# A streaming encoder layer: the first stage rebuilt, with shifts and scales by quarters and the index keys made in it

## Chip, cores and metric

One core of a Trainium2 chip runs the whole program. The metric is the device time of one execution in microseconds (us). Before the change it is 1277.1 us, the median of 3 runs (1276.33 to 1277.18).

## What is computed

One encoder layer over 1024 prompt tokens and 32 sample tokens (together T = 1056), D_MODEL = 1024, all in float32:

```python
mod = silu(c) @ w_ada + b_ada                    # per stream: c_prompt or c_sample
shift, scale, gate = split(mod, 3)
h = rms_norm(x, g_norm) * (1 + scale) + shift
z = h @ w_in                                     # q k v gate_a iq iw ik glu gate_b merge
score = sum_heads(w * relu(iq . ik))             # indexer; top-k keys per query
y_a = (attention over the selected keys * silu(gate_a)) @ w_a
y_b = (silu(layer_norm(depthwise_conv(ga * sigmoid(gb)))) * silu(gate_b)) @ w_b
x = x + gate * ((sigmoid(m_a) * y_a + sigmoid(m_b) * y_b) @ w_out)
```

followed by a last RMSNorm; k, v, ik and the conv state are outputs too. The indexer has 8 heads of 64 (iq, 512 columns of `w_in`), 64 columns of keys (ik) and 8 of weights (iw).

## The kernel before

All matrix products of the layer itself are made from pairs of rounded float32 numbers: an operand is split into a high part (`hh`, `wh`) and the rest (`hl`, `wl`), and three matmuls, hh.wh, hl.wh and hh.wl, replace one (`mm3`, L129 to L132). Everything of `z` is laid out with features on partitions and the 1056 tokens on columns.

**First stage** (L218 to L438). It makes hh and hl, 8 blocks j of 128 features by 1056 tokens, and the indexer's queries. x comes as 9 token tiles (`load_x`, L240). A tile is squared and summed (ACT, `sq_x`), its root and reciprocal are made (`scale_x`, L295: up to three tiles share the small steps), it is scaled in place (L313 on ACT, L315 on DVE or POOL), transposed in eight 128x128 pieces (`trans_x`, L320, into two PSUM banks `tx`) and copied to `xT` (L333).

Shift and scale are products of a vector with `w_ada`. `mod` (L345) goes by halves q of 512 features, by i (shift or scale) and by k (8 blocks of the contraction): 32 pieces, each with a stationary of 4 columns (`scf`) and 512 moving columns. 20 of them are float32 matmuls (L355); 12 are first split by `mod_pre` (L341, L342) and run as two rounded matmuls (L352, L353). `mod_out` (L361) turns the rows by transposes (L365) and leaves shift and scale per feature in `AB`.

```python
        nc.gpsimd.tensor_scalar(h, x, AB[:, j, 2:3], AB[:, j, 0:1], op0=OP.mult, op1=OP.add)
        nc.scalar.activation(hi, x, AF.Identity, bias=AB[:, j, 0:1], scale=AB[:, j, 2:3])
        nc.vector.tensor_sub(lo, h, f32(hi))
```

This is `h_of` (L374 to L379): for each block j and each of three parts of the tokens (f: 0 to 255, i: 256 to 767, t: 768 to 1023) h is made on POOL (L377), its rounded value on ACT (L378) and the rest on DVE (L379): 24 calls. `iq_mm` (L391) makes the queries of the first two of four 128-column blocks of iq, each in columns 256 to 767 (512 wide) and 768 to 1055 (288 wide).

The order of all this is written out by hand in two strings of steps: `LOADS` (L76) is the order in which SP issues the transfers, `ORDER` (L80) the order of the compute steps. PE, DVE and ACT run their instructions exactly in the order of the program; POOL's and SP's instructions are put in order by a scheduler. `LOADS` takes w_ada in pieces of 128 or 256 rows by 512 columns; 4 buffers hold x tiles, 4 hold blocks of w_ada.

**After the first stage** `iq_out` (L509) empties the queries from PSUM, `first_w` (L528) splits the weights of the index keys, and `Jobs` (L551) runs a list of products (L1363) one behind the other: the keys and iw (72 columns, `idx_done`), iq blocks 2 and 3, then K, V and all the other columns of `w_in`, most through `proj` (L538, matmuls L545). Between the k blocks of a job, `step` (L487) pops one small piece of other work: transposes, score products (`dots`), the convolution, the top-k search.

Of the kernel before, what the change touches and what calls it, by code (L numbers as in the profile page):

```python
# [107 lines left out]
def _build(tc, nc, a, o, top):  # L108
# [141 lines left out]
    iqraw = None  # L250
    for op, *i in LOADS:
        if op == "x":
            load_x(*i)
        elif op == "a":
            load_ada(*i)
        elif op == "q":
            iqraw = load_w([(w_in, C_IQ, 256)])
        else:
            ikraw = load_w([(w_in, C_IK, 64), (w_in, C_IW, 8)])

    rest = tl(stp, [128, 512], BF, "junk")
    nc.vector.memset(rest, 0.0)
    psS, psS_st = pool("psS", space=PSUM)
    p = tl(psS, [128, 512], F, "iq00")
    for i in range(WARM):
        nc.tensor.matmul(p, rest[:, 0:128], rest, start=True, stop=True)
    nc.vector.memset(scf, 0.0)
# [4 lines left out]
    nc.scalar.activation(sc, p.rearrange("p (s k) -> p k s", s=2), AF.Silu)  # L272
    bg_ = tl(stp, [128, 24], F, "bg_")

    def bias():
        p = misc([128, 24])
        nc.tensor.transpose(p, brow, ident[:24, :24])
        nc.vector.tensor_copy(bg_, p)
        nc.vector.tensor_scalar(bg_[:, 8:16], bg_[:, 8:16], 1.0, None, op0=OP.add)

    nc.gpsimd.memset(f32(scz), 0.0)

    IQC = ((0, 512), (512, NIQ - 512))
    iqps = {0: {}, 1: {}}
    xT = tl(stp, [128, KD, T], F, "xT")

    sums = {}
# [7 lines left out]
    def scale_x(tiles):  # L295

        w = len(tiles)
        v, sq, r, t = [tl(stp, [128, 3], F, n, 2) for n in ("vv", "rs_s", "rs_r", "rs_t")]
        v, sq, r, t = v[:, :w], sq[:, :w], r[:, :w], t[:, :w]
        if 8 in tiles:  # L300
            yield lambda: nc.vector.memset(v, 1.0)
        for c, i in enumerate(tiles):
            yield lambda c=c, i=i, n=tok(i): nc.vector.tensor_scalar(v[:n, c:c + 1], sums[i][:n], 1.0 / D, EPS,
                                                                     op0=OP.mult, op1=OP.add)
        yield lambda: nc.scalar.activation(sq, v, AF.Sqrt)
        yield lambda: nc.vector.reciprocal(r, sq)
        yield lambda: nc.vector.tensor_mul(t, r, r)
        yield lambda: nc.vector.tensor_mul(t, t, v)
        yield lambda: nc.vector.tensor_scalar(t, t, -0.5, 1.5, op0=OP.mult, op1=OP.add)
        yield lambda: nc.vector.tensor_mul(r, r, t)  # L310
        for c, i in enumerate(tiles):
            if XENG[i] == 2:
                yield lambda c=c, i=i, n=tok(i): nc.scalar.mul(xn[i][:n], xn[i][:n], r[:n, c:c + 1])  # L313
                continue
            yield lambda c=c, i=i, n=tok(i), e=(nc.vector, nc.gpsimd)[XENG[i]]: e.tensor_scalar(  # L315
                xn[i][:n], xn[i][:n], r[:n, c:c + 1], 1.0, op0=OP.mult, op1=OP.mult)
# [1415 lines left out]
```

## Time and profile before

| | |
|---|---|
| median of 3 runs | 1277.1 us |
| the profiled execution | 1275.99 us |
| its span, first to last instruction | 1274.2 us |
| PE busy | 1250.3 us (98%) |
| PEld (weight loads) | 1176.6 us (92%) |
| DVE busy | 900.2 us (71%) |
| ACT busy | 617.6 us (48%) |
| POOL busy | 196.0 us (15%) |
| granted TensorE clock, mean | 0.997 of full |

PE is the matrix engine, PEld its weight loads, DVE the vector engine, ACT the scalar engine, POOL GpSimd, SP the engine that issues most DMAs. "Busy" counts an engine from an instruction's start to its end; a matmul's end is modelled, and two that follow one another overlap, so the distance from one start to the next is what a matmul costs. A shape such as `128*72 128x352` is a stationary of 128 rows by 72 columns and an output of 128 partitions by 352 columns as the profile prints it.

### The profile page before, as it was taken

The numbers are of one execution on the slowest core, as the hardware profiler recorded it, in microseconds if no ns is written. First come the engines' busy times: TensorE is split into PE (matmuls) and PEld (weight loads), VectorE is DVE, ScalarE is ACT, GpSimd is POOL, SyncE is SP. The second block draws the span as 40 slices with busy tenths as digits, with TensorE's granted clock in tenths as the row PEclk, the third lists the DMA queues.
The fourth block names the chain that finished last, engine by engine and source line by source line (L and its number), as shares of the span: only waits on it lengthen the run. The fifth ranks groups of instructions, "written<-read, shape, count | busy, mean of one in ns | idle before, by whom it ended". The sixth has DMA issues, their size and how long they took to land.

```text
span 1274.2 us, 19148 instructions
## 1 busy us (share of the span) xinstructions
PE 1250.3 (98%) x7434; PEld 1176.6 (92%) x7434; DVE 900.2 (71%) x1435; ACT 617.6 (48%) x1142; POOL 196.0 (15%) x289
## 2 busy tenths in 40 slices
PE   7999999999999999999999999999999999999997
PEld 2589999999999999999999999999998889998785
DVE  4855547878898898879885558853258888775554
ACT  5645444566766666677213343341236776123322
POOL 3740111000000000100000000000023353311222
PEclk9999999999999999999999999999999999999998
DMA  9431222121222122221322421257123335645131
GB/s 339 138 102 50 85 68 85 51 102 52 72 80 68 69 68 85 75 78 52 117 103 102 164 107 41 79 174 267 56 75 88 96 108 193 204 150 176 65 133 67
DMA packets 110395, 136.38 MB, mean 107 GB/s; under 512 B 10667, under 2 KB 87715, under 8 KB 110176
## 3 DMA queue, kind: packets, MB, share of 16 engines
q1 hardware_dynamic: 99232, 100.62, 24.9%
q10 hardware_dynamic: 5872, 19.48, 3.8%
q0 software_dynamic: 5200, 15.05, 3.6%
q8 instruction: 58, 0.95, 0.3%
q14 instruction: 33, 0.27, 0.1%
HBM read 98.60 MB, written 36.54 MB: 106 GB/s over the span
## 4 chain that ended last, share of the span: by engine, by line
PE 94%; DMA 2%; POOL 1%; DVE 1%; ACT 1%; issue 0%; SPq 0%; ACTq 0%; DVEq 0%
PE proj L545 70%; PE PT L1284 2%; PE y L132 2%; PE y L130 2%; PE y L131 2%; PE O L130 1%; PE O L132 1%; PE O L131 1%; PE misc L743 1%; PE misc L744 1%; POOL h L377 1%; DMA ada<-in_w_ada_dram 1%; PE misc L132 1%; PE misc L131 1%; DMA xt<-in_x_prompt_dram 1%; PE misc L130 1%
## 5 line engine op out<-in xcount | busy, mean ns | idle before, releaser
L967 DVE SCALAR_TENSOR_TENSOR s<-u,vec,s 128x1086 f32<-128x1086 f32 x240 | 314.5, 1347 | 2.6
L545 PE MATMUL proj<-hh,wh 128*128 128x352 f32 x1440 | 312.8, 325 | 0.0
L545 PE MATMUL proj<-hh,wl 128*128 128x352 f32 x1440 | 310.3, 323 | 0.0
L545 PE MATMUL proj<-hl,wh 128*128 128x352 f32 x1440 | 309.8, 323 | 0.0
L545 PEld LDWEIGHTS proj<-hh,wh 128*128 128x128 f32 x1440 | 245.1, 189 | 1.9
L545 PEld LDWEIGHTS proj<-hh,wl 128*128 128x128 f32 x1440 | 246.8, 188 | 0.0
L545 PEld LDWEIGHTS proj<-hl,wh 128*128 128x128 f32 x1440 | 244.6, 188 | 0.0
L813 ACT ACTIVATE relu<-scores,cand 128x384 bf16<-128x384 f32 (+6 forms) x224 | 183.8, 823 | 72.2 <-DVE cand L828 69.5
L127 DVE TENSOR_TENSOR wl<-raw,wh 128x1024 fp32r<-128x1024 f32 (+1 forms) x84 | 100.7, 1202 | 79.8 <-ACT wh L126 78.6
L126 ACT CAST wh<-raw 128x1024 fp32r<-128x1024 f32 (+1 forms) x84 | 86.0, 1027 | 55.5 <-PE proj L545 43.8
L746 ACT ACTIVATE relu<-misc 128x384 f32<-128x384 f32 (+3 forms) x80 | 40.0, 524 | 63.4 <-PE misc L744 62.1
L757 DVE SCALAR_TENSOR_TENSOR scores<-relu,iws,scores 128x384 f32<-128x384 f32 (+3 forms) x70 | 43.7, 655 | 34.4 <-ACT relu L746 34.4
L126 ACT CAST u<-PT 128x512 fp32r<-128x512 f32 (+2 forms) x76 | 43.2, 572 | 45.0 <-PE PT L1284 42.6
L127 DVE TENSOR_TENSOR u<-PT,u 128x512 fp32r<-128x512 f32 (+2 forms) x76 | 50.6, 671 | 14.7 <-ACT u L126 14.3
L906 ACT ACTIVATE s<-proj 128x1056 f32<-128x1056 f32 x24 | 25.3, 1053 | 67.9 <-PE proj L545 67.9
L813 ACT ACTIVATION_READ_ACCUMULATOR relu<-scores,cand 128x1 f32 x224 | 42.4, 189 | 0.0
L545 PE MATMUL proj<-oa,wh 128*128 128x352 f32 x192 | 41.2, 323 | 0.0
L1264 POOL TENSOR_SCALAR E<-E,st 128x1024 f32<-128x1024 f32 (+4 forms) x36 | 33.7, 935 | 41.9 <-DVE st L1263 21.0
L545 PE MATMUL proj<-u,wh 128*128 128x352 f32 x192 | 38.6, 322 | 0.0
L1259 ACT ACTIVATE E<-E,st 128x1024 f32<-128x1024 f32 (+4 forms) x36 | 34.7, 964 | 7.9 <-DVE st L1252 7.8
L938 POOL DMA_DIRECT2D out_dram<-cvo x8 | 4.1, 517 | 216.5 <-ACT cvo L937 216.5
L888 POOL DMA_DIRECT2D mask_d<-relu x7 | 3.8, 549 | 209.2 <-ACT relu L887 209.2
(447 smaller groups left out, 2120.7 us busy)
## 6 DMA issues: line engine op xcount, KB each, us to landing
raw<-in_w_in_dram SPq DMA_DIRECT2D x24, 1024.0 KB, 5.3
raw<-in_w_in_dram SPq DMA_DIRECT2D x16, 512.0 KB, 5.1
ada<-in_w_ada_dram SPq DMA_DIRECT2D x24, 256.0 KB, 5.8
sma_d<-s ACTq DMA_DIRECT2D x8, 528.0 KB, 2.7
smb_d<-s ACTq DMA_DIRECT2D x8, 528.0 KB, 2.7
ga_d<-s ACTq DMA_DIRECT2D x8, 528.0 KB, 2.7
qh_d<-s ACTq DMA_DIRECT2D x8, 528.0 KB, 2.7
ql_d<-s SPq DMA_DIRECT2D x8, 528.0 KB, 2.8
```

What stands on the lines that cost most here:

```text
L126: nc.scalar.copy(hi, src)
L127: nc.vector.tensor_sub(lo, src, f32(hi))
L130: nc.tensor.matmul(out, ah, bh, start=first, stop=False)
L131: nc.tensor.matmul(out, ah, bl, start=False, stop=False)
L132: nc.tensor.matmul(out, al, bh, start=False, stop=last)
L545: nc.tensor.matmul(p[:n, c, :CH], a_[:, k, :n], b_(k, c), start=first, stop=last)
L746: nc.scalar.activation(r[:, :n], p[:, :n], AF.Relu, scale=0.125)
L757: nc.vector.scalar_tensor_tensor(acc, r[:, :n], w, acc, op0=OP.mult, op1=OP.add)
L813: nc.scalar.activation(scr[:, :s.shape[1]], s, AF.Sign, bias=f32(hold["cand"])[:, i:i + 1], accum_out=cnt[:, i:i + 1])
L967: nc.vector.scalar_tensor_tensor(d[:, :DW], u[:, k:k + DW], wj[:, k:k + 1], d[:, :DW], op0=OP.mult, op1=OP.add)
L1259: nc.scalar.activation(e, e, AF.Exp, bias=mn, scale=-1.0, accum_out=st[:, 1:2])
L1264: nc.gpsimd.tensor_scalar(e, e, st[:, 2:3], 1.0, op0=OP.mult, op1=OP.mult)
```

## The change

The first stage is written anew; what comes after it is the same but for the first jobs.

- Shift and scale go by quarters q of 256 features. One moving row holds 256 shift and 256 scale columns, and `w_ada` comes in eight blocks of 1 MB (q, g), each by two DMAs with rows of 1 KB. `mod` runs 8 groups of four float32 matmuls. Each of the four has a stationary of 32 columns (2 in use, the others zero) and writes another 32 partitions of one PSUM bank, with another k block. `mod_row` copies the bank, `mod_cols` sums the four parts and turns the rows by four matmuls with the 0/1 matrix `sel`. `mod_pre` and its splits are gone.
- h of the outer tokens (t and f) is made in one call for blocks 2 to 7 (part `tf`), so there are 18 parts instead of 24, and h may be made on DVE ("D") or POOL ("P").
- The index keys are made in the first stage (`k_mm`), in three parts of 352 columns, from weights that are loaded and split there. The second block of the queries (iq 1) leaves the stage and becomes the first job.
- Every instruction group is a step of `ORDER`. New steps `z:n` run n matmuls of zeros (`idle`); 21 in all.
- The root, the reciprocal and the scaling are done tile by tile.

```diff
-    def load_ada(q, i, k0, n=4):
+    def load_ada(q, g):
+        t = ada[q, g] = tl(stp, [128, 4, 2, 256], F, "ada", 4)
+        for i in range(2):
+            c = D * i + 256 * q
+            nc.sync.dma_start(t[:, :, i], w_ada[512 * g:512 * g + 512, c:c + 256].rearrange("(k p) c -> p k c", p=128))
-            nc.tensor.matmul(out, sch[:, k, :], h, start=k == 0, stop=False)
-            nc.tensor.matmul(out, scz[:, k, :], l, start=False, stop=k == KD - 1)
-        else:
-            nc.tensor.matmul(out, scf[:, k, :], ada[q, i, k], start=k == 0, stop=k == KD - 1)
+    def mod(q, g):
+        if g == 0:
+            pm[q] = tl(psS, [128, 512], F, "acc")
+        for j in range(4):
+            nc.tensor.matmul(pm[q][32 * j:32 * j + 32], scp[:, 4 * g + j, :], ada[q, g][:, j].rearrange("p i c -> p (i c)"),
+                             start=g == 0, stop=g == 1)
+    def mod_cols(q):
+        p = pm[q] = misc([128, 2, 2, 2])
+        for i in range(2):
+            for c in range(2):
+                nc.tensor.matmul(p[:, i, c, :], mrow[q][:, 256 * i + 128 * c:256 * i + 128 * c + 128], sel[:, 0, 0:2],
+                                 start=True, stop=True)
+    def h_of(p, j, e):
...
+        ENG[e].tensor_scalar(h, x, AB[:, j, 2:3], AB[:, j, 0:1], op0=OP.mult, op1=OP.add)
+    def k_mm(k, c):
+        wh, wl, _ = iqw["k"]
+        out, z = ikp[:72, c, :CH], slice(CH * c, CH * c + CH)
+        mm3(out, wh[:, k, :], wl[:, k, :], hh[:, k, z], hl[:, k, z], *turn_of("k", c))
+    def idle(n):
+        for i in range(n):
+            nc.tensor.matmul(ikp[:, 0, :], rest[:, 0:128], rest, start=True, stop=True)
...
-    iq_out(0, (0,))
-    first = first_w()
-    iq_out(0, (1,))
-    iq_out(1)
+    iq_out(0)
...
-    jobs = [("w", [(w_in, C_IK, 64), (w_in, C_IW, 8)], [(0, 72, idx_done)], 1, hrows),
+    jobs = [("w", None, [(0, 128, 1)], 1, hrows),
...
-    cache_ik()
-    side.append(cache_kT)
-    Jobs(jobs, first).run()
+    jobs = Jobs(jobs, iqw[1])
+    jobs.load(1)
+    load_caches()
+    idx_done(ikp)
+    side.extend([cache_ik, cache_kT])
```

Of the two strings one line each (`x:8` loads tile 8, `a:0,1` the block q=0, g=1 of w_ada; `m` is `mod`, `t` and `c` a transposed half tile and its copy, `h`, `i`, `l` the three operations of h, `q` and `k` queries and keys by block and part):

```diff
-x:2 a:0,0,0,1 x:3 a:0,1,0,1 a:0,0,4,1 a:0,1,4,2 x:4 x:8 x:5 a:1,0,0,1 x:7 a:1,1,0,2 x:6 a:1,0,4,1 q a:1,1,4,1 x:0
+x:8 x:2 x:3 x:4 a:0,0 x:5 a:0,1 x:6 k x:7 a:1,0 a:1,1 q:0 x:0 a:2,0 x:1 a:2,1 a:3,0 a:3,1 q:1
...
+m:1,0 c:7,0,A l:i,0 i:t,0 h:t,0,P wd:k i:t,1 h:t,1,P z:1 m:1,1 l:t,0 k:1,1 a:1,D wa:0 k:0,1 l:t,1 k:0,2 o:1 wd:0
```

**PE, the middle of the first stage.** Before (`misc<-ada,scf` is a float32 piece of shift or scale, `ah` and `al` a split one, `tx<-ident,xt` a tile's transposes):

```order
L327 MATMUL tx<-ident,xt 128x128 x8
L365 MATMUL misc<-ident,h 128x4 x8
L355 MATMUL misc<-ada,scf 4x512
L352 MATMUL misc<-ah,sch 4x512
L353 MATMUL misc<-al,scz 4x512
L355 MATMUL misc<-ada,scf 4x512 x2
```

and now, from the transposes of tile 7 on (`acc<-ada,scp` is one group of four, `ik<-rest` a matmul of zeros, `ik<-hh,wkh` a third of the keys of one block):

```order
L342 MATMUL misc<-ident,xt 128x128 x8
L355 MATMUL acc<-ada,scp 32x512 x4
L453 LDWEIGHTS rest
L453 MATMUL ik<-rest 128x512
L355 MATMUL acc<-ada,scp 32x512 x4
L130 MATMUL ik<-hh,wkh 72x352
L131 MATMUL ik<-hl,wkh 72x352
L132 MATMUL ik<-hh,wkl 72x352
```

The pieces come in groups of four on four sets of partitions, and the first keys stand right behind the second quarter's second group.

**PE, the end of the first stage.** Before:

```order
L130 MATMUL iq_603<-hh,wh 128x288
L131 MATMUL iq_603<-hl,wh 128x288
L132 MATMUL iq_603<-hh,wl 128x288
L646 MATMUL misc<-ident,s 64x128 x2
L545 MATMUL proj_849<-hh,s_772 72x352 x3
L545 MATMUL proj_849<-hl,s_772 72x352 x3
L545 MATMUL proj_849<-hh,s_773 72x352 x3
```

and now:

```order
L130 MATMUL ik<-hh,wkh 72x352
L131 MATMUL ik<-hl,wkh 72x352
L132 MATMUL ik<-hh,wkl 72x352
L130 MATMUL proj_808<-hh,wh 128x512
L131 MATMUL proj_808<-hl,wh 128x512
L132 MATMUL proj_808<-hh,wl 128x512
```

The transposes of the cached index keys (L646) no longer stand between the stage and the first job; that job is now iq block 1, and the 72 matmuls of the keys (`proj_849`) are gone from behind the stage.

**POOL, the first stage.** Before, from the splits of w_ada (`al`) to the parts of h:

```order
L342 TENSOR_TENSOR al<-ada,ah 128x512 x7
L377 TENSOR_SCALAR h<-xT,AB 128x512 x2
L342 TENSOR_TENSOR al<-ada,ah 128x512
L377 TENSOR_SCALAR h<-xT,AB 128x512
L315 TENSOR_SCALAR xt<-xt,rs_r 128x1024
L315 TENSOR_SCALAR xt<-xt,rs_r 32x1024
```

and now, from the scaling of tiles 2, 4 and 7 on (`hs` are the 32 sample tokens of a quarter):

```order
L333 TENSOR_SCALAR xt<-xt,rs_r,rs_t 128x1024 x3
L392 TENSOR_SCALAR h<-xT,AB 128x512
L403 TENSOR_TENSOR hs<-xT,AB 128x64
L404 TENSOR_TENSOR hs<-hs,AB 128x64
L405 CAST hh<-hs 128x2x32
L406 TENSOR_TENSOR hl<-hs,hh 128x2x32
L392 TENSOR_SCALAR h<-xT,AB 128x256 x2
```

The eight splits are gone; POOL makes 12 parts of h in place of 24, and the sample's parts of three quarters.

## Rows read from the trace of the kernel before

**Rows 1.** The page: busy time and share of the span, and the chain by engine.

```profile
PE 1250.3 (98%) x7434; PEld 1176.6 (92%) x7434; DVE 900.2 (71%) x1435; ACT 617.6 (48%) x1142; POOL 196.0 (15%) x289
...
PE 94%; DMA 2%; POOL 1%; DVE 1%; ACT 1%; issue 0%; SPq 0%; ACTq 0%; DVEq 0%
```

**Rows 2.** Stretches: length; busy us (instructions) of PE, PEld, DVE, ACT, POOL; PEclk, DMA share, GB/s.

```profile
0.00:10.00 10.00, 2.38 (x4) 0.47 (x4) 2.51 (x11) 5.02 (x10) 3.74 (x29) 1.00 0.77 252
10.00:20.00 10.00, 9.07 (x28) 3.13 (x29) 6.32 (x16) 2.96 (x6) 1.34 (x2) 1.00 1.06 368
20.00:30.00 10.00, 9.81 (x39) 2.99 (x38) 6.18 (x18) 8.59 (x17) 5.60 (x5) 1.00 1.03 388
30.00:40.00 10.00, 8.23 (x38) 2.64 (x36) 7.77 (x19) 5.58 (x9) 7.92 (x7) 1.00 0.91 320
...
60.00:70.00 10.00, 8.51 (x49) 7.11 (x47) 5.74 (x14) 6.30 (x13) 9.94 (x13) 1.00 0.04 8
```

**Rows 3.** The chain in order of time: start, length, what.

```profile
52.46 4.88 POOL h L377 x4
...
59.78 6.01 POOL h L377 x7
...
68.54 1.83 DMA s<-in_cache_idx_k_dram
...
73.03 10.13 PE proj L545 x63
```

**Rows 4.** The same stretches' view: only rows of 256 floats move from 47 to 49.

```profile
43.00:46.00 3.00, 3.00 (x13) 1.28 (x12) 3.00 (x5) 0.58 (x3) 0.00 (x0) 1.00 0.72 121
47.00:49.00 2.00, 2.00 (x18) 1.75 (x17) 1.51 (x12) 1.75 (x6) 0.56 (x1) 1.00 1.05 372
```

**Rows 5.** PE in order of time: start, length, line, shapes, [idle before, releaser].

```profile
41.11 3.60 PE L355 MATMUL misc<-ada,scf 128*4 128x512 f32 x8
44.64 1.29 PE L327 MATMUL tx<-ident,xt 128*128 128x128 f32 x8
...
49.00 0.39 PE L132 MATMUL iq<-hh,wl 128*128 128x512 f32 x1
49.23 0.40 PE L130 MATMUL iq<-hh,wh 128*128 128x512 f32 x1
...
61.41 0.29 PE L130 MATMUL iq<-hh,wh 128*128 128x288 f32 x1
61.54 0.29 PE L131 MATMUL iq<-hl,wh 128*128 128x288 f32 x1
...
70.41 0.41 PE L646 MATMUL misc<-ident,s 128*64 128x128 f32 x2 [1.42 <-DMA s<-in_cache_idx_k_dram]
...
72.37 0.66 PE L654 MATMUL misc<-ident,s 128*128 128x128 f32 x4
...
82.99 0.39 PE L130 MATMUL proj<-hh,wh 128*128 128x512 f32 x1
```

**Rows 6.** Groups by line and shape from 0 to 84 us: busy, mean ns, idle before.

```profile
L377 POOL TENSOR_SCALAR h<-xT,AB 128x256 f32<-128x256 f32 x16 | 13.5, 854 | 5.7 <-ACT xT L333 5.7
L342 POOL TENSOR_TENSOR al<-ada,ah 128x512 fp32r<-128x512 f32 x8 | 10.5, 1321 | 18.6 <-DVE ah L341 9.9 <-ACT ah L341 6.7 <-PE misc L355 1.9
...
L377 POOL TENSOR_SCALAR h<-xT,AB 128x512 f32<-128x512 f32 x8 | 9.4, 1176 | 2.5 <-DVE vv L303 2.1 <-DVE hl L387 0.4
...
L293 ACT ACTIVATE junk<-xt 128x1024 bf16<-128x1024 f32 x8 | 8.4, 1053 | 5.6 <-DMA xt<-in_x_prompt_dram 5.5
...
L379 DVE TENSOR_TENSOR hl<-h,hh 128x512 fp32r<-128x512 f32 x8 | 5.8, 735 | 0.6 <-POOL h L377 0.6
...
L315 POOL TENSOR_SCALAR xt<-xt,rs_r 128x1024 f32<-128x1024 f32 x2 | 2.8, 1395 | 0.7 <-DVE rs_r L310 0.7
```

**Rows 7.** DVE, and last POOL, in order of time: one line alone and beside POOL.

```profile
10.12 0.75 DVE L315 TENSOR_SCALAR xt<-xt,rs_r 128x1024 f32<-128x1024 f32 x1
...
26.89 1.87 DVE L315 TENSOR_SCALAR xt<-xt,rs_r 128x1024 f32<-128x1024 f32 x1
...
26.91 4.21 POOL L342 TENSOR_TENSOR al<-ada,ah 128x512 fp32r<-128x512 f32 x3 [1.94 <-PE misc L355]
```

More of the change, by code (lines that the diff above doesn't have):

```diff
@@ L249, in _build @@
     nc.scalar.dma_start(brow[16:24], fold(a["g_norm"]))
-    iqraw = None
+    ikraw, iqraw = [tl(wpool, [128, KD, 256], F, "raw", 2) for i in range(2)]
     for op, *i in LOADS:
@@ L255, in _build @@
             load_ada(*i)
-        elif op == "q":
-            iqraw = load_w([(w_in, C_IQ, 256)])
-        else:
[L259 to L267, printed above, removed]
-    warm = tl(stp, [128, 1], F, "warm")
@@ L269, in _build @@
-    nc.scalar.activation(warm, rest[:, 0:1], AF.Silu)
-    p = misc([128, 16])
-    nc.tensor.transpose(p, crow, ident[:16, :16])
[L272 to L287, printed above, removed]
-    def sq_x(i):
-        n = tok(i)
-        ss = sums[i] = tl(stp, [128, 1], F, "ss", 4)
-        scr = tl(stp, [128, D], BF, "junk")
-        nc.scalar.activation(scr[:n], xn[i][:n], AF.Square, accum_out=ss[:n])
[L295 to L316, printed above, removed]
@@ L439, in _build @@
-    stp_st.close()
+        elif op == "k":
+            for c, c0, n in ((0, C_IK, 64), (64, C_IW, 8)):
+                nc.sync.dma_start(ikraw[:, :, c:c + n], w_in[:, c0:c0 + n].rearrange("(k p) c -> p k c", p=128))
+        else:
+            c = 128 * i[0]
+            nc.sync.dma_start(iqraw[:, :, c:c + 128], w_in[:, C_IQ + c:C_IQ + c + 128].rearrange("(k p) c -> p k c", p=128))
     idv = ident.rearrange("p (a b) -> p a b", a=4)
@@ L446, in _build @@
         nc.gpsimd.tensor_copy(sel[:, i], sel[:, 0])
+    rest = tl(stp, [128, 512], BF, "rest")
+    nc.vector.memset(rest, 0.0)
+    psS, psS_st = pool("psS", space=PSUM)
+    for tag in ("acc", "iq0", "iq1"):
+        tl(psS, [128, 512], F, tag)
+    ikp = tl(psS, [128, 3, 512], F, "ik")
+    scp = tl(stp, [128, KD, 32], F, "scp")
+    nc.vector.memset(scp, 0.0)
+    warm = tl(stp, [128, 1], F, "warm")
+    nc.scalar.activation(warm, rest[:, 0:1], AF.Silu)
+    p = misc([128, 16])
+    nc.tensor.transpose(p, crow, ident[:16, :16])
@@ new lines, in iq_mm, with turn_of @@
+    def iq_mm(t, w, ks, cs=(0, 1), first=None, last=None):
+        for k in ks:
+            for c in cs:
+                u, n = IQC[c]
+                cols = slice(IQ0 + u, IQ0 + u + n)
+                mm3(iqps[t][c][:, :n], w[0][:, k, :], w[1][:, k, :], hh[:, k, cols], hl[:, k, cols],
+                    k == 0 if first is None else first, k == KD - 1 if last is None else last)
+    made = {}
+    def turn_of(*key):
+        made[key] = made.get(key, 0) + 1
+        return made[key] == 1, made[key] == KD
@@ L449, in _build @@
+    for op, *i in ORDER:
+        order[op](*i)
+    stp_st.close()
     upool, upool_st = pool("upool")
@@ L526, in iq_out @@
         nc.gpsimd.tensor_copy(iqs[64:128, 2 * t + 1, :], f32(d[0:64, z]))
-    def first_w():
-        h, l = [slot8(FR)[:, :KD * 72].rearrange("p (k n) -> p k n", k=KD) for i in range(2)]
-        split(ikraw[:, :, :72], h, l)
-        return h, l
-    iq_out(0, (0,))
-    first = first_w()
-    iq_out(0, (1,))
-    iq_out(1)
+    iq_out(0)
     def proj(w, rows, n, npop, mid):
@@ L611, in run @@
             step(0)
-    psS_st.close()
-    psA, psA_st = pool("psA", space=PSUM)
     onesr = tl(big, [128, 128], FR, "onesr")
@@ L1381, in _build @@
     jobs += yb[:3] + [("call", prelude)] + yb[3:]
-    cache_ik()
-    side.append(cache_kT)
-    Jobs(jobs, first).run()
+    jobs = Jobs(jobs, iqw[1])
[3 more added lines that the diff above has]
+    side.extend([cache_ik, cache_kT])
+    psS_st.close()
+    psA, psA_st = pool("psA", space=PSUM)
+    jobs.run()
     pop(1000)
```

261 lines of the change are left out of this document (129 added, 132 removed).

## The prediction

> **What bounds the kernel now.** I read the page first. PE is busy 98% of the span and 94% of the chain is PE [rows 1], so nearly everywhere the time is the sum of PE's work, and only a stretch in which PE waits or does needless work can give time back. The view by stretches shows where that is: for the first 40 us DMA runs at 250 to 390 GB/s while PE is busy with slow small pieces, and from 60 to 70 POOL is busy for 9.94 us of 10 and DMA stands still [rows 2]. The chain in order of time names POOL's h (L377) as what ends last there, from 52.5 to 68.5, then a load of cached keys, and then pure PE work [rows 3]. So the first stage is bound by transfers up to about 40 us, then by POOL, and PE gets its dense stream only at 70.4 us, at L646; the first piece that both kernels have left to do behind it, iq block 2, starts at 82.99 [rows 5]. From there on the program is the same in both. I take what the change is worth as the shift of that point.
>
> **What the change does to each engine.** *POOL*: it loses 8 splits (10.5 us) and half of its 24 parts of h (22.9 us); what is left is 9 x 1.18 + 3 x 0.85 = 13.2 us [rows 6] and some small sample steps. It stops being the bound. *DVE* takes six parts of h and loses splits; I cost that at nothing as long as PE has work that is ready, and price the other case below. *SP and DMA*: the same megabytes in rows of 1 KB instead of 2 KB. Rows of 1 KB alone ran at 372 GB/s [rows 4], against 388 at best [rows 2], so nothing is lost. The key weights, 0.29 MB in rows of 256 and 32 bytes, now stand in the middle of the queue; at the 121 GB/s of the stretch that held them [rows 4] they take 2.4 us, 1.6 more than at full speed. The loads wait for buffers as before, four of x and four of w_ada, and each is given back by PE steps that run well before its turn.
>
> *PE, removed*: 20 float32 pieces, each two records, eight records in 3.5 us [rows 5], so 0.88 us a piece and 17.6 in all; 12 split pieces of two matmuls at 0.23 (49.00 to 49.23), 5.6 us. *Added*: 8 groups of four float32 pieces. This is the unknown price. Nothing in the trace of before writes four column parts at once. If the four overlap wholly, a group costs one piece, 0.88 us; if not at all, 3.53 us. Neither end is excluded. I take 1.2 us, near the lower end: the row of L355 shows 0.44 us a record for a stationary of 4 columns, twice the 0.23 of a rounded matmul with all 128 columns and the same 512 moving ones [rows 5]; so time there goes by what streams, not by columns that are filled, and the four parts fill different columns. The Trainium skill (TensorE: Matmul & The Clock Gate, Part 3) gives 2.38 times for three column parts side by side; if four gained in proportion, 3.53 / 3.17 = 1.1 us, an estimate. No row here shows it.
>
> *Moved in*: the keys, 72 matmuls at 10.13 / 63 = 0.161 us [rows 3], 11.6 us. *Moved out*: iq block 1, 8 x (3 x 0.2325 + 3 x 0.13) = 8.7 us [rows 5]. *Matmuls of zeros*: 21 x 0.23 = 4.9 us; 20 stand ahead of the second quarter, where PE waits for transfers anyway, so only the one behind is counted. They can't raise the clock: it is granted at 1.00 in every stretch already [rows 2].
>
> **The sum.** (a) *When PE's work becomes dense.* Ahead of m:1,0 the queue brings x 8 and 2 to 7, two blocks of w_ada, the key weights and its own block: 0.13 + 6 x 0.52 + 3 x 1.05 + 0.29 = 6.7 MB. 2.5 MB are there at 10 us and 6.2 at 20 [rows 2]; the rest and the 1.6 us make 23, and I add 1.5 us for the landing. Ahead of it on PE are tile 7's transposes, which wait for its square (1.05), root and reciprocal (about 0.8, an estimate) and scaling on POOL (1.4) [rows 6]. ACT and DVE also serve tile 6 and the first h there, so I say 26 us. (b) *PE's work from m:1,0 to the end of the stage*: 6 groups x 1.2 = 7.2; keys 11.6; iq block 0 8.7; four half tiles of transposes, 8 in 1.05 (44.64 to 45.69 by the next start), 2.1; turning three quarters 1.5, bounded by the 0.6 that eight small transposes took before and 2; one matmul of zeros 0.2. Sum 31.3 us, end at 57.3. (c) *Waits in it*: 2 us, between none and the 1.8 us in 10 that PE stood still from 30 to 40 [rows 2] (5 us). The last shifts need 13.5 MB, which at these rates land at about 42 us, some 3 us before PE comes to them (13.4 us of its work lie behind). End of the stage: 59.3. (d) *From there to iq block 2*: 0.3 us for PSUM, iq block 1 8.7, the two cache transposes 0.41 and 0.66 [rows 5]: 69.4 us. The score products that the new job pops early are done once in either kernel and cancel.
>
> 82.99 - 69.4 = 13.6 us gained. The profiled execution took 1276.0 us (span 1274.2), so it would take 1262.4; the median of the runs lies 1.1 above it, which gives **1263.5 us**. What is late next is PE itself: from 26 us on it has hardly a gap to close.
>
> **Rivals.** *The two passes of a piece block the next piece* (0.17). A float32 piece leaves two records, 40 for 20 pieces. If matmuls start strictly in order, the second pass of part 1 waits for the first in the same columns, and part 2's first can only start with it: five slots of 0.44, 2.2 us a group. The Trainium skill (the same page and part) says that matmuls keep program order in start and end; by that rule the price is this one. One microsecond more on six groups, and about half of it on the first two, which lie partly in waits: 6.9 us, 1270.4 us. For it speaks that every row of PE here starts in order; against it that weight loads already run beside matmuls (PEld is busy 92% of the span [rows 1]), so the array does hold parts of two matmuls at once.
>
> *The four parts do not overlap, or changing between array shapes costs as much* (0.08): 3.53 us a group, 2.33 x 6.9 = 16 us more, of which 13.6 are the gain: **slower**, 1279.5 us. It decides from 3.2 us a group on. The Trainium skill (TensorEngine Tiling (Array Packing), Key Properties) says that a change of the tiling mode drains the engine; it gives no price, and each group brings two changes.
>
> *POOL and DVE hinder each other* (0.09). The same scaling took 0.75 us on DVE alone and 1.87 while POOL ran splits [rows 7]. Behind the last shifts stand one h and six rests (hl, mean 0.735) on DVE, three h and the sample's steps on POOL; with 0.5 us more on each of eight, on the path because the last queries and keys wait for them, 4 us and the same stretch of the third quarter partly hidden: 1268. For it: before, DVE ran L379 in 0.735 on average beside a busy POOL, so part of it is in the prices already; against it, PE has ready work of quarters two and three to do meanwhile.
>
> *The gain is given back* (0.04), because something behind the stage, the loads of w_in or DVE's convolution (71% busy), sets the pace: 1277, no change. PE's 94% of the chain speaks against it.
>
> **Chances and range.** My forecast has 0.62, with 1259 to 1268 as its own range: 0.88 us a group takes 2.2 off, no waits 2 more, 5 us of waits instead of 2 adds 3, and 1.5 us on the guess of 26 either way. The range of 1258 to 1273 takes in blocked passes and hindrance at their prices, 0.62 x 0.95 + 0.15 + 0.09 = 0.83. A measurement of this kernel tells 0.2%, 2.6 us, from no change. Faster by more: the forecast, blocked passes (a little of it lost), hindrance: 0.87. Within: 0.05. Slower: 0.08.
>
> **What would show it.** Right: in the changed trace a group of L355 starts its four parts within about 1.2 us; POOL well under half busy from 26 to 60; PE without gaps of a microsecond from 26 us on; iq block 2's first matmul near 69 us plus the score products popped before it; behind that the same rows as now, 13 to 14 us earlier. Blocked passes show as the eight records of a group spread over 2.2 us, no overlap as 3.5. Hindrance shows as L398 (hl) or h far above 0.735 with PE waiting on them. The forecast is wrong if the shift at the first job of K, which starts at the same work in both, is under 9 or over 18 us, or if it shrinks further on.

## The result, and the profile after

| | before | after |
|---|---|---|
| median of the runs compared | 1276.71 us (4 runs) | 1260.82 us (4 runs, 1260.2 to 1261.92) |
| ratio | | 0.9877, 95% interval 0.986 to 0.9894 |
| the profiled execution | 1275.99 us | 1260.89 us |
| its span | 1274.2 us | 1259.1 us |
| granted clock, mean | 0.997 | 0.997 |

The change makes the kernel 15.9 us faster by these medians; 1263.5 was forecast, with 1258 to 1273 as the range. In a second comparison on another occasion the ratio was 0.9885 (0.987 to 0.99), 14.6 us.

The page of after: busy time and share of the span, and the chain by engine (before: [rows 1]).

```profile
PE 1240.1 (98%) x7471; PEld 1178.1 (94%) x7471; DVE 892.3 (71%) x1423; ACT 612.6 (49%) x1132; POOL 180.6 (14%) x282
...
PE 96%; DVE 1%; ACT 1%; POOL 1%; DMA 1%; issue 0%; ACTq 0%; POOLq 0%; DVEq 0%
```

PE is busy for 10.2 us less, and it stands still for 19.0 us of the span in place of 23.9. Together that is the 15.1 us by which the span is shorter. The matmuls of zeros count as busy here, 8.2 us, so of what the kernel needs PE does more than 10.2 us less. Stretches of ten microseconds of after, with the columns of [rows 2]:

```profile
0.00:10.00 10.00, 4.59 (x17) 2.01 (x18) 3.51 (x16) 7.73 (x15) 3.70 (x29) 1.00 0.78 269
10.00:20.00 10.00, 8.12 (x45) 5.41 (x46) 5.91 (x17) 3.38 (x10) 1.19 (x1) 1.00 1.10 334
20.00:30.00 10.00, 9.17 (x65) 4.57 (x64) 7.97 (x20) 8.82 (x16) 5.09 (x8) 1.00 1.10 347
30.00:40.00 10.00, 9.94 (x65) 6.71 (x63) 7.66 (x20) 4.78 (x9) 4.79 (x7) 1.00 1.08 355
...
50.00:60.00 10.00, 9.77 (x57) 8.09 (x55) 7.92 (x13) 6.21 (x11) 8.09 (x11) 1.00 0.11 23
60.00:70.00 10.00, 9.30 (x58) 8.39 (x59) 6.55 (x15) 5.08 (x8) 3.31 (x8) 1.00 0.46 143
```

Up to 30 us nothing is gained: PE stands still for 8.1 us there, 8.7 before, and matmuls of zeros fill a part of the rest. Transfers run at 334 to 347 GB/s from 10 us on, below the 368 and 388 of before [rows 2]. They are not what the second quarter waits for last: its first group stands on PE behind tile 7's transposes, and these wait for POOL's scaling of that tile (25.93). The gain lies between 30 and 70 us, where PE was 8.23 and 8.51 of 10 us busy [rows 2] and POOL 9.94; now PE is full, and POOL's busiest stretch is 50 to 60 with 8.09. PE of after in order of time, the rows that answer to [rows 5]:

```profile
25.93 1.09 PE L342 MATMUL misc<-ident,xt 128*128 128x128 f32 x8 [0.30 <-POOL xt L333]
26.95 1.06 PE L355 MATMUL acc<-ada,scp 128*32 128x512 f32 x8
...
45.82 1.06 PE L355 MATMUL acc<-ada,scp 128*32 128x512 f32 x8
46.81 0.38 PE L130 MATMUL ik<-hh,wkh 128*72 128x352 f32 x1
...
48.33 0.95 PE L367 MATMUL misc<-sel,mrow 128*128 128x2 f32 x8
49.13 0.36 PE L130 MATMUL ik<-hh,wkh 128*72 128x352 f32 x1
...
59.58 0.32 PE L132 MATMUL ik<-hh,wkl 128*72 128x352 f32 x1
60.70 0.47 PE L130 MATMUL proj<-hh,wh 128*128 128x512 f32 x1 [0.80 <-DVE s L535]
...
71.24 0.39 PE L130 MATMUL proj<-hh,wh 128*128 128x512 f32 x1
```

From one start to the next a group of four pieces takes 0.99 us (45.82 to 46.81), and a single piece took 0.88. The second quarter's first group stands at 26.95, the last key at 59.58, and the first job starts at 60.70 after a wait of 0.96 us (a key costs 0.16). Iq block 2 starts at 71.24 in place of 82.99.

Inside one group, by the records of L355 alone in stretches of 0.05 us (busy and number of instructions of PE, then of PEld):

```profile
45.80:45.85 0.05, 0.03 (x4) 0.03 (x5) 1.00 0.85 266
...
46.20:46.25 0.05, 0.05 (x4) 0.00 (x0) 1.00 0.62 205
46.25:46.30 0.05, 0.05 (x8) 0.00 (x0) 1.00 0.58 184
```

Four records are there in the first 0.05 us and four more come in from 46.25 on: all four parts make their first pass together, for about 0.45 us, and then their second.

### The profile page after: what moved, and what is told of

The parts are those of the page before. It is cut to its first block, busy times and chain, and to the rows that moved or that the text cites. A ratio compares the mean times of both kernels' runs of the same rounds, so it can differ in the third digit from the quotient of the medians.

```text
span 1259.1 us, 19159 instructions
## 1 busy us (share of the span) xinstructions
PE 1240.1 (98%) x7471; PEld 1178.1 (94%) x7471; DVE 892.3 (71%) x1423; ACT 612.6 (49%) x1132; POOL 180.6 (14%) x282
## 4 chain that ended last, share of the span: by engine, by line
PE 96%; DVE 1%; ACT 1%; POOL 1%; DMA 1%; issue 0%; ACTq 0%; POOLq 0%; DVEq 0%
PE proj L552 70%; PE PT L1291 2%; PE y L132 2%; PE y L130 2%; PE y L131 2%; PE O L130 1%; PE O L132 1%; PE O L131 1%; PE misc L750 1%; PE misc L751 1%; PE misc L132 1%; PE misc L131 1%; PE misc L130 1%; PE proj L130 1%; PE proj L131 1%; PE proj L132 1%
## 5 line engine op out<-in xcount | busy, mean ns | idle before, releaser
L127 DVE TENSOR_TENSOR wl<-raw,wh 128x1024 fp32r<-128x1024 f32 (+1 forms) x82 | 97.9, 1196 | 72.2 <-ACT wh L126 72.0
L127 DVE TENSOR_TENSOR u<-PT,u 128x512 fp32r<-128x512 f32 (+2 forms) x76 | 50.6, 671 | 14.5 <-ACT u L126 14.1
L1677 ACT ACTIVATE x<-yv 128x512 f32<-128x512 f32 (+2 forms) x19 | 11.6, 609 | 49.1 <-DVE yv L1676 49.1
```

Source lines behind the costliest of these rows:

```text
L127: nc.vector.tensor_sub(lo, src, f32(hi))
```

## The experiments

"K" in the table is the start of the first matmul of the first K job. What lies ahead of it is the same work in all of these kernels but for the pairs of score products popped there (9 in before, 13 in after and its variants). In before, and then in after:

```profile
104.81 0.65 PE L545 MATMUL proj<-hh,wh 128*128 128x352 f32 x3
```

```profile
93.38 0.64 PE L552 MATMUL proj<-hh,wh 128*128 128x352 f32 x3
```

The rest of the span behind K is 1165.7 to 1165.9 us in every row but the last two. Behind the first row, the time of the kernel before was 1275.45 to 1275.74 in these comparisons, so the ratios compare across them.

| kernel | median us | of before, 95% | K, us |
|---|---|---|---|
| after, first time | 1260.82 | 0.9877 (0.986 to 0.9894) | 93.38 |
| after, again | 1261.1 | 0.9885 (0.987 to 0.99) | 92.89 |
| one column part | 1279.73 | 1.0032 (1.002 to 1.0044) | 112.26 |
| two column parts | 1266.46 | 0.9929 (0.9914 to 0.9943) | 98.88 |
| no zeros | 1262.44 | 0.9898 (0.9883 to 0.9913) | 94.99 |
| first six zeros out | 1262.73 | 0.9897 (0.9882 to 0.9912) | 95.03 |
| only the first six | 1262.89 | 0.9898 (0.9882 to 0.9915) | 95.42 |
| keys behind | 1269.24 | 0.9954 (0.9937 to 0.997) | 100.50 |
| all h on POOL | 1263.11 | 0.9905 (0.9889 to 0.9922) | 94.66 |
| end, first try | 1260.72 | 0.9885 (0.987 to 0.99) | 92.89 |
| end, second try | 1260.18 | 0.9877 (0.9862 to 0.9891) | 92.51 |
| tiles where they were | 1262.77 | 0.9901 (0.9885 to 0.9918) | 93.17 |
| before, again | 1275.34 | 1.0001 (0.999 to 1.0013) | 103.97 |

### One column part, and two

```diff
-            nc.tensor.matmul(pm[q][32 * j:32 * j + 32], scp[:, 4 * g + j, :], ada[q, g][:, j].rearrange("p i c -> p (i c)"),
-                             start=g == 0, stop=g == 1)
+            nc.tensor.matmul(pm[q][0:32], scp[:, 4 * g + j, :], ada[q, g][:, j].rearrange("p i c -> p (i c)"),
+                             start=g == 0 and j == 0, stop=g == 1 and j == 3)
```

> The four float32 pieces of a group add up in the same 32 partitions instead of four sets of 32; everything else stays. Theory A (PE's work sets the end of the stage, and a group costs 1.00 us only because the four parts run side by side): a group's eight records spread over about 3.5 us, 2.5 us more each. Six groups behind 26 us count in full, 15 us, and the two ahead of it lie partly in waits, up to 3 more: 1275 to 1280 us, the whole gain gone; iq block 2 near 87 us. Theory B (transfers, POOL and DVE set the stage's end, PE has room): at most 4 us, 1261 to 1265. Theory C (the short stationary of 32 columns is what makes a group cheap, not where it writes): still about 1 us a group, 1261.

The other kernel writes `pm[q][c:c + 32]` with `c = 32 * (j % 2)`, starts with `j < 2` and stops with `j > 1`; `mod_row` and `mod_cols` take 32 and 64 partitions.

> The four pieces of a group write two sets of 32 partitions, two pieces in each, one behind the other. Theory A (pieces that write different sets overlap wholly, those in the same set not at all): two rounds of 0.88 and a little, 1.9 us a group, 0.9 more than with four sets; 5.4 us on six groups and up to 1 on the other two: 1266 to 1267 us. Theory B (the stage has room on PE): 1261 to 1262. If changing from one piece to the next costs by itself, the group takes over 2.3 us and the time is above 1269.

A group of one part, PE in order of time:

```profile
45.78 3.62 PE L355 MATMUL acc<-ada,scp 128*32 128x512 f32 x8
...
79.58 0.47 PE L130 MATMUL proj<-hh,wh 128*128 128x512 f32 x1 [0.81 <-DVE s L535]
```

and of two parts:

```profile
46.26 1.91 PE L356 MATMUL acc<-ada,scp 128*32 128x512 f32 x8
```

By the length of their rows, 3.62, 1.91 and 1.06 us for one, two and four parts: pieces of the same part follow one another, those of different parts run side by side, and the short stationary alone makes nothing cheaper (theory C falls). K moves by 18.9 and 5.5 us; 1279.73 and 1266.46 are the times that theory A gave (with one part iq block 2 starts at 90.12, 3 us behind the 87 that it named). Theory B falls: PE's work sets the end of the stage. Without the overlap the new stage, with everything else that the change brought, is 4 us slower than the old one, so without it there is no gain.

### Without the matmuls of zeros

All `z` steps leave `ORDER`, 21 matmuls; nothing else moves.

```diff
-sq:8 s:8 v:8 sq:2 r:8 x:8,D s:2 v:2 sq:3 z:6 t:8,1 r:2 t:8,0 x:2,P s:3 v:3 c:8,1,A r:3 sq:4 z:1 t:2,1 x:3,D c:2,1,D
+sq:8 s:8 v:8 sq:2 r:8 x:8,D s:2 v:2 sq:3 t:8,1 r:2 t:8,0 x:2,P s:3 v:3 c:8,1,A r:3 sq:4 t:2,1 x:3,D c:2,1,D
```

> The 21 matmuls of zeros are taken out, nothing else. Theory A (they do nothing for the time, since 20 stand where PE waits and the granted clock reads 1.00 throughout): 0.2 us less by the one that stands behind 26 us, and a little more where one in front delays a transpose by 0.2: 1260 to 1261 us. Theory C (they keep the array at its full rate: the first six start 0.43 us apart, those from 15.55 on 0.22): the transposes and the first two groups of shifts then take up to twice as long until about 20 us; two groups 2 us and transposes some 4 us more, of which about half lies in waits for x: 1262 to 1265 us, and the first h comes later by that.

Stretches of two microseconds; the column behind POOL is the granted clock:

```profile
16.00:18.00 2.00, 0.00 (x0) 0.00 (x0) 0.51 (x3) 1.86 (x5) 0.00 (x0) 1.00 1.11 298
18.00:20.00 2.00, 1.44 (x10) 1.11 (x11) 1.60 (x4) 0.66 (x3) 0.00 (x0) 0.95 1.03 357
20.00:22.00 2.00, 2.00 (x12) 0.59 (x10) 0.69 (x1) 1.97 (x5) 0.00 (x0) 0.50 1.10 349
...
26.00:28.00 2.00, 1.28 (x7) 1.08 (x6) 1.90 (x2) 2.00 (x4) 2.00 (x3) 0.66 1.10 349
28.00:30.00 2.00, 2.00 (x13) 0.89 (x15) 2.00 (x4) 1.18 (x3) 1.78 (x4) 0.50 1.07 356
```

and PE there:

```profile
20.73 1.94 PE L354 MATMUL acc<-ada,scp 128*32 128x512 f32 x8
...
28.82 2.51 PE L354 MATMUL acc<-ada,scp 128*32 128x512 f32 x16
```

Theory C holds for the size and the cause, not for the place. PE stands still for 2.5 us around 17 us, the granted clock falls to 0.50 (1.2 GHz) from 20 to 22 and again from 28 to 30, and the second group takes 1.94 us in place of 1.06; the first group, which theory C counted as slowed too, keeps 1.07. K comes 1.6 us later, and the time is 1262.44, 1.3 and 1.6 us above the two medians of after. In after, the clock is 1.00 in all these stretches. So the zeros do hold the clock. Which of them?

> Only the first six matmuls of zeros (2.8 to 5.5 us) are taken out. Theory A (a fall of the granted clock comes from the gaps between 15 and 27 us, and the first six stand too far ahead of them; the transposes at 9.94 take 0.23 us each with or without them): the clock stays at 1.00 to 30 us, and the time is that of the changed kernel within 0.5 us. Theory B (PE has to be busy from early on to reach the full clock in time for the first shifts): the first group of shifts takes 2 us instead of 1, and the stage ends 1 us or more later.

> The other 15 matmuls of zeros are taken out, and the first six stay. Theory A (those 15 hold the clock over the gaps): as with all 21 out, the granted clock is at 0.50 for some 3 us twice between 19 and 30 us, iq block 2 starts 1.6 us later and the time is 1.6 to 2.6 us above the changed kernel. Theory B: the time of the changed kernel within 0.5 us, and the clock at 1.00.

First six out, then (second fence) only the first six left:

```profile
18.00:20.00 2.00, 0.90 (x6) 0.69 (x7) 1.74 (x5) 1.08 (x3) 0.00 (x0) 0.88 1.00 346
20.00:22.00 2.00, 2.00 (x12) 1.50 (x15) 0.48 (x2) 1.12 (x2) 0.00 (x0) 0.50 1.08 353
22.00:24.00 2.00, 1.68 (x9) 0.11 (x2) 1.04 (x3) 1.97 (x5) 0.00 (x0) 0.77 1.09 349
```

```profile
20.00:22.00 2.00, 2.00 (x13) 0.62 (x12) 0.69 (x1) 1.84 (x5) 0.00 (x0) 0.57 1.10 352
...
28.00:30.00 2.00, 1.99 (x10) 0.92 (x12) 2.00 (x4) 1.49 (x3) 1.78 (x4) 0.50 1.05 357
```

With only the first six, the clock is low from 20 to 30 us, K is 2.0 us later than in the first trace of after: the 15 zeros in the gaps are needed, as theory A of that run said. But with only the first six out the clock falls too, once, and K is 1.65 us later. Theory A of that run falls; theory B gives the size, but not the place, since the first group keeps its 1.06 us and the loss comes at 20 us. In that execution x 5 also came later: ACT takes its square at 16.65 us, 16.11 in after, and only then copies what the second half of tile 4 needs, which PE transposes at 18.65 in place of 18.11. That made PE's gap in front 1.95 us in place of 1.30. All four runs lie between 1262.62 and 1262.94, so the loss is not that of one execution; whether the six are missed by themselves or through that gap stays open.

### The keys behind everything else

All 24 `k` steps stand at the end of `ORDER`, in the same order among themselves.

```diff
-k:1,2 O:1 q:0,1 q:1,1 h:i,2,D i:i,2 h:i,3,P q:0,0 i:i,3 l:i,2 S:1,P q:1,0 sq:0 l:i,3 q:2,0 k:2,1 v:0 s:0 q:3,0 r:0
+O:1 q:0,1 q:1,1 h:i,2,D i:i,2 h:i,3,P q:0,0 i:i,3 l:i,2 S:1,P q:1,0 sq:0 l:i,3 q:2,0 v:0 s:0 q:3,0 r:0
```

> All 24 key steps (72 matmuls) are moved from between the queries and shifts to the end of the stage. Theory A (the keys of the first three quarters are the work that PE does while the last shifts and h are made): the 12 key steps that now stand ahead of the last quarter's first h, 12 x 0.48 = 5.8 us, become waiting, and about half of the last quarter's 2.9 us too; the 0.96 us wait at the stage's end goes: 4 to 8 us more, 1265 to 1269. Theory B (queries and transposes alone keep PE full, and the keys cost the same wherever they stand): 1260 to 1261.

```profile
44.00:46.00 2.00, 1.25 (x11) 0.35 (x4) 1.71 (x8) 0.99 (x2) 1.28 (x2) 1.00 1.05 331
46.00:48.00 2.00, 1.89 (x11) 1.26 (x10) 1.08 (x2) 2.00 (x4) 2.00 (x3) 0.90 0.27 85
48.00:50.00 2.00, 1.72 (x6) 1.09 (x5) 1.97 (x6) 1.43 (x3) 1.91 (x3) 0.50 0.00 0
50.00:52.00 2.00, 2.00 (x6) 1.48 (x6) 1.90 (x4) 2.00 (x4) 1.94 (x3) 0.50 0.02 4
```

K is 7.1 us later and the median 1269.24: theory A, at its upper end. The stretches of 2 us show that part of it is again the clock: PE waits for the last shifts, the clock falls to 0.50 from 48 to 54, and the queries of the last quarter run at half rate. So the keys in after's places save the wait that they fill and, here, also the fall of the clock behind it.

### All parts of h on POOL

The six `h` steps with `D` take `P`.

```diff
-h:f,0,P h:tf,3,D t:1,1 i:tf,3 l:tf,2 m:3,0 i:f,0 l:tf,3 q:2,1 i:f,1 k:2,2 l:f,0 k:3,0 c:1,1,A h:f,1,D l:f,1 q:3,1
+h:f,0,P h:tf,3,P t:1,1 i:tf,3 l:tf,2 m:3,0 i:f,0 l:tf,3 q:2,1 i:f,1 k:2,2 l:f,0 k:3,0 c:1,1,A h:f,1,P l:f,1 q:3,1
```

> The six parts of h that DVE makes go to POOL, which then makes all 18; the sample's steps stay. Theory A (POOL is near its limit at the stage's end already: busy 8.09 of 10 us from 50 to 60, and the last h on it ends the chain there): 0.96 us for the part in the last quarter, and 0.5 to 2 us that the second and third quarter push on: 2 to 4 us more, 1263 to 1265. Theory B (as in the prediction, POOL is well under half busy and PE has ready work meanwhile): no more than 0.5 us, 1261. Theory C (hindrance: DVE and POOL slow each other, and fewer parts on DVE let both run faster): below 1260.

The median is 2.0 us above after's second one. K is 1.8 us later than in the second trace of after, whose second quarter started within 0.07 us of this one's (26.45 and 26.38 us), and 1.3 later than in the first. That is theory A, at its lower end. So the parts that DVE took over matter, and POOL in after isn't free. Theories B and C fall.

### The end of the stage

First try: `wa:1` and `wd:1` (the split of iq block 1's weights) move into a gap ahead, and `h:tf,6` goes to DVE.

```diff
-k:2,0 O:2 m:3,1 h:i,5,P S:2,D k:3,2 h:i,4,P a:3,A k:1,0 i:i,4 h:tf,4,P k:0,0 o:3 i:tf,4 l:i,4 h:tf,5,P i:tf,5 l:tf,4
+k:2,0 O:2 m:3,1 h:i,5,P wa:1 S:2,D wd:1 k:3,2 h:i,4,P a:3,A k:1,0 i:i,4 h:tf,4,P k:0,0 o:3 i:tf,4 l:i,4 h:tf,5,P i:tf,5 l:tf,4
...
-h:tf,7,P q:5,0 i:tf,6 l:i,6 k:5,2 h:tf,6,P q:7,0 l:tf,7 wa:1 q:6,0 l:tf,6 k:6,1 wd:1 q:7,1 k:5,0 q:6,1 k:6,2 k:7,1
+h:tf,7,P q:5,0 i:tf,6 l:i,6 k:5,2 q:7,0 h:tf,6,D l:tf,7 q:6,0 l:tf,6 k:6,1 q:7,1 k:5,0 q:6,1 k:6,2 k:7,1
```

> Two edits at the end of the stage: the weights of iq block 1 are split in the gap of ACT and DVE at 45 to 48 us instead of between the last rest of h and the emptying of the queries, and the last part of h (block 6, outer tokens) is made on DVE instead of POOL. Theory A (the 0.96 us wait ahead of the first job, and the 0.3 us wait of the last queries, come from DVE's 1.3 us of splitting and POOL's late h): both waits go, about 1.1 us less, 1259.7 us, too little for the times alone, so the trace decides: the first job starts within 0.2 us of the last key, near 59.7 us. Theory B (the first job waits for something else, the PSUM banks' last reader on ACT or a transfer): the wait stays at 0.8 to 1 us and the time at 1260.8.

PE of this kernel at the end of the stage:

```profile
59.88 0.32 PE L132 MATMUL ik<-hh,wkl 128*72 128x352 f32 x1
60.03 0.40 PE L130 MATMUL proj<-hh,wh 128*128 128x512 f32 x1
```

its POOL where the split now stands on DVE:

```profile
45.56 5.04 POOL L392 TENSOR_SCALAR h<-xT,AB 128x512 f32<-128x512 f32 x4 [3.12 <-DVE AB L376]
```

and POOL of after in the same place:

```profile
45.57 3.10 POOL L392 TENSOR_SCALAR h<-xT,AB 128x512 f32<-128x512 f32 x4 [3.12 <-DVE AB L376]
...
50.90 1.50 POOL L392 TENSOR_SCALAR h<-xT,AB 128x512 f32<-128x512 f32 x1
```

The wait of the first job is gone, as theory A had it, but the queries still wait 0.24 us and the last key comes 0.3 us later than in after (59.88 against 59.58), so that half of the gain is left (K 0.5 us sooner) and the median shows nothing. Where DVE's split (1.23 us) now stands, with the rests (hl) close behind it, POOL's four h took 1.94 us longer, about the split and one rest (0.7) together. In after one h beside DVE's rests took 1.50 us, again about one rest more than the 0.78 of each of four beside DVE's small steps of the sample. The Trainium skill (GPSIMD Engine Reference, Specifications) says that POOL shares its way to SBUF with VectorE and contends with instructions that have two SBUF inputs; the split and hl are of that kind, and these rows agree.

Second try: `h:tf,6` on DVE as above, `wd:1` out of `ORDER`, and the split behind the emptying of the queries, where POOL makes no h:

```diff
     iq_out(0)
+    w_lo(1)
```

> The end of the stage again: DVE splits the weights of iq block 1 behind the emptying of the queries instead of ahead of it, and makes the last part of h (block 6, outer tokens) in POOL's place. Theory A (what the first job waits for is DVE's emptying, and the earlier split failed since it stood beside POOL's four parts of h, which then took 5.04 us instead of 3.10): the first job starts near 59.7 us without a wait, its third matmul may wait up to 0.5 us for the split; about 0.8 us less than the changed kernel, 0.06%, which the trace must show, since the times alone hardly can. Theory B (POOL's chain of the last quarter sets the end wherever the split stands): no change.

```profile
59.37 0.40 PE L129 MATMUL proj<-hh,wh 128*128 128x512 f32 x1
59.61 0.39 PE L130 MATMUL proj<-hl,wh 128*128 128x512 f32 x1
60.27 0.50 PE L131 MATMUL proj<-hh,wl 128*128 128x512 f32 x1 [0.27 <-DVE wl L446]
```

K is 0.87 us sooner than in the first trace of after (whose second quarter started within 0.07 us of this one's), 1260.18 us against 1261.1 on the same chip, with four runs from 1260.11 to 1260.25 and 1260.38 to 1262.42. That is theory A's size, and the fastest version here; against after it is 0.07%, less than such a comparison tells surely.

### Behind the stage: the kernels again, and where the tiles lie

The shift between the traces of before and after is 13.2 us at 278 us, when all 80 score products are done in both, and 15.1 at the end. What adds 1.9 us to a part of the program that is the same?

> The changed kernel itself once more, beside the variants on the same chip, so that they can be held against it and not only against the kernel before. All theories: 0.9877 of the kernel before, within its interval of 0.986 to 0.9894; from 326 us on its stretches were 0.1 to 0.2% shorter than those of the kernel before (159.7 against 160.0 us); if that belongs to one execution and not to the change, it will not be there again, or with another size.

> The kernel before itself, for a trace from the chip that ran the variants. In its first trace a full job of 72 matmuls takes 11.65 us (266.35 to 278.00), in the changed kernel and in every variant 11.63. Theory A (that is the execution or the chip, not the change): now 11.63 here too, the span near 1273 us, and behind 340 us the shift between the two kernels stays at about 13.3 us. Theory B (the change makes the later jobs faster by 0.2%, by where its tiles lie): 11.65 again, and the shift grows from 13.3 to 15 us.

ACT's emptying of two neighbouring full jobs, in before as it ran again:

```profile
616.58 1.06 ACT L906 ACTIVATE s<-proj 128x1056 f32<-128x1056 f32 x1 [9.11 <-PE proj L545]
628.23 1.05 ACT L906 ACTIVATE s<-proj 128x1056 f32<-128x1056 f32 x1 [9.15 <-PE proj L545]
```

and in after:

```profile
615.05 1.05 ACT L913 ACTIVATE s<-proj 128x1056 f32<-128x1056 f32 x1 [9.12 <-PE proj L552]
626.68 1.06 ACT L913 ACTIVATE s<-proj 128x1056 f32<-128x1056 f32 x1 [9.13 <-PE proj L552]
```

11.65 and 11.63 us again, and from K to the end this run of before takes 1169.4 us (1273.4 less 103.97), as its first did (1274.2 less 104.81). So theory A of the last run falls: the two kernels differ by 0.2% in these jobs, and it belongs to the change. The chip isn't it: this run of before was made on another chip than after's second one and the variants, and so was the kernel below, but before took 1275.45 to 1275.74 us beside each of them. The change also made a constant tile smaller and dropped two, by which all tiles behind them lie 320 bytes a partition lower. The last kernel is after with that undone:

```diff
-    scf = tl(cst, [128, KD, 2], F, "scf")
+    scf = tl(cst, [128, KD, 4], F, "scf")[:, :, 0:2]
     AB = tl(cst, [128, KD, 4], F, "AB")
+    pad = tl(cst, [128, 2, KD, 4], F, "pad")
+    nc.gpsimd.memset(pad, 0.0)
```

> The changed kernel with one thing undone: the small constant tiles are given the size that they had before (two unused ones of 128 bytes a partition and a scf twice as wide), so that every tile behind them, the weights wh, wl and raw among them, lies 320 bytes a partition further on, where it lay in the kernel before. A full job of 72 matmuls takes 11.65 us in the kernel before, on two occasions, and 11.63 in the changed kernel and all variants. Theory A (where the tiles lie makes the matmuls of the later jobs 0.2% faster): 11.65 us again, and some 1.7 us more than the changed kernel, about 0.9898 of the kernel before. Theory B (it is something else that the change moved): 11.63, and 0.9885.

```profile
615.77 1.05 ACT L915 ACTIVATE s<-proj 128x1056 f32<-128x1056 f32 x1 [9.15 <-PE proj L554]
627.42 1.05 ACT L915 ACTIVATE s<-proj 128x1056 f32<-128x1056 f32 x1 [9.15 <-PE proj L554]
```

11.65 us: theory A. From K to the end this kernel takes 1167.4 us (1260.6 less 93.17), after 1165.7: 1.7 us. Its median is 1.7 us above after's second one. ACT empties the same two jobs at 278.00 and 843.01 us in before, at 264.81 and 828.52 in after and at 264.70 and 829.70 here: against this kernel the shift stays at 13.3 us, against after it grows from 13.2 to 14.5. So 1.7 of the 1.9 us are the place of the tiles, which no part of the change was about. Why 320 bytes matter to a matmul was not looked into.

## Why the prediction was right, and where it was not

**Bound and place.** Right: PE is the bound, the gain is made in the first stage, and column parts (18.9 us of K without them), the keys' places (7.1) and the relief of POOL (1.8 for six parts of h) make it. No run put POOL's eight splits back by themselves. What is behind the stage keeps the gain.

**(a) 26 us for the second quarter.** 26.95 in the first trace, 26.45 in the second, and 26.7 to 26.9 in four variants that leave this stretch as it is. Up to a microsecond late, and by what the prediction named: tile 7's square, root and scaling on ACT, DVE and POOL. The half microsecond between the two traces is x 5's: ACT waits for its transfer until 16.11 us in the first and 15.60 in the second.

**(b) PE's work, 31.3 us.** From 26.95 to 59.74 PE is busy 32.48 us. The disputed price, 1.2 us a group, is 1.00 by starts, near the lower end that the row of the small stationary had pointed to; that takes 1.2 us off. Turning a quarter, priced 0.5 us, takes 0.8 to 0.9 (48.33 to 49.13), which gives 1.1 us back on three. Keys and queries take 12.2 and 9.2 us by starts, waits between them included, where their closest spacing had given 11.6 and 8.7: another 1.2 us.

**(c) Waits of 2 us, end at 59.3.** PE stands still for 0.31 us in these 32.79, and ends at 59.74. That the end is met within half a microsecond is in part luck: 1.0 from (a), 1.1 from the turning, 1.2 from keys and queries and 0.4 from the rest stand against 1.2 from the groups and the 2 us of waits. That DVE's extra parts cost little fits: the kernels with one more of them did not lose by it. What they cost by themselves no run shows. "POOL well under half busy" did not hold: it is busy 19.63 of the 32.79 us, and 8.09 from 50 to 60. It stopped being the bound by less than the prediction thought, as the kernel with all h on POOL shows. And "nothing is lost" with rows of 1 KB did not hold: from 10 to 40 us the queue moved 334 to 355 GB/s, where before had moved 368 and 388 from 10 to 30 us [rows 2]. No run separates these rows from the still shorter ones of the key weights and queries beside them. The kernel with the keys behind waits for the last block of w_ada until 43.83 us, where the prediction had the last shifts landed at about 42:

```profile
43.83 1.07 PE L354 MATMUL acc<-ada,scp 128*32 128x512 f32 x8 [0.17 <-DMA ada<-in_w_ada_dram]
```

After comes to that block at 45.82, so there it cost nothing.

**(d) 0.3 us of PSUM wait, iq block 2 at 69.4.** Mis-sized: the wait is 0.96 us, DVE's split and emptying ahead of it. Iq block 2 starts at 71.24, 0.8 us of it nine small transposes in three groups and a pair of score products that the job pops before. So this point is 1.0 us later than forecast: 0.44 by the stage's end, 0.66 by the wait.

**Shift and time.** 13.6 us were forecast; 13.2 at 278 us, by when both kernels have done the same. At K the shift is 11.4 us (104.81 to 93.38), inside the 9 to 18 that the prediction allowed; after has done four more pairs of score products there. The profiled execution took 1260.9 where 1262.4 was forecast: 0.4 us too little in the stage, 1.9 more behind it, of which 1.7 are the tiles' place. The sentence that failed there is "behind that the same rows as now". The last 1.2 us of the 2.7 between forecast and median: the prediction put the median 1.1 above the profiled execution as in before, and in after they are equal.

**The zeros, costed at nothing.** For the forecast they were rightly no gain, but "they can't raise the clock: it is granted at 1.00 in every stretch already" read the wrong kernel. In before, PE's small pieces filled the stretch from 10 to 30 us (9.07 and 9.81 of 10 [rows 2]). The column parts shorten that work by 2.5 us in each of two groups (3.62 against 1.06) and gaps open; without zeros the clock falls to half behind them, which the runs show. That the removed pieces had held it in before is how I read the two stretches; no run put them back alone.

**Rivals.** Blocked passes (2.2 us a group): refuted, four parts start their first passes together and a group takes 1.00 us. The Trainium skill (TensorE: Matmul & The Clock Gate, Part 3) says that matmuls keep program order in start and end; read as both passes of a piece ahead of the next piece, as the prediction read it, that is not what these rows show, and the measurement decides. No overlap, and drains between array shapes: refuted at that size; beyond its two passes of 0.44 a group costs some 0.1 us. The price was right, the condition wasn't met: 1279.5 us were forecast for no overlap, and one column part, which has none, takes 1279.73. Hindrance of POOL and DVE: real (5.04 against 3.10 us), but after's order keeps most of it off the path; hl took 0.770 us on average against 0.735 [rows 6]. Gain given back: no, it grew.

## What to carry to other kernels

Price what a change takes away as cover too, and not only as work: where shorter pieces leave gaps, TensorE's clock can fall, and here 21 matmuls of zeros, 8.2 us of PE's busy time that lies nearly all in waits, save some 1.6 us. Small float32 products whose results can stand on different sets of 32 partitions are worth spreading over all four, and one profile of a single group settles whether they overlap. When a later part of a program that was not touched runs at another pace, look also at where its tiles lie.

## What the runs showed of the hardware

- *Parts.* Float32 pieces of 128x512 with 32 columns cost 3.62, 1.91 and 1.06 us for four in one, two and four column parts.
- *Clock.* After PE had stood still (2.5 us without the zeros, 2.7 with only the first six) the granted clock was 0.50 for some 3 and some 10 us, and a group took 1.94 us in place of 1.06. The column misses the low level in the first microseconds: in after it reads 1.00, while six zeros take 2.74 us at first, and three take 0.66 (15.55 to the next row's start) later. In the kernel with the tiles put back it reads 0.50 from 10 to 14 us, and eight transposes there take 1.91 us, the same as in after.

```profile
2.79 2.74 PE L453 MATMUL ik<-rest 128*128 128x512 bf16 x6
...
15.55 0.82 PE L453 MATMUL ik<-rest 128*128 128x512 bf16 x3
16.21 0.60 PE L342 MATMUL misc<-ident,xt 128*128 128x128 f32 x4
```

- *Places.* 320 bytes a partition in where operands lie changed the jobs of 352 columns by 0.2%, 11.63 to 11.65 us a job, in three traces with the one place and in all that were read with the other. This holds up to about 840 us; behind that the two kernels' matmuls of 352 columns keep pace (shift 14.5 us at 843 and at 1156).
- *POOL beside DVE.* One scaling of 128x512 on POOL takes 0.78 us beside DVE's small steps of the sample and 1.50 beside DVE's subtractions of two tiles, about one such subtraction (0.7) more.
